# Loads and low parts reordered, the second norm in halves on PSUM, and sums formed in steps further apart, in a one-layer encoder kernel

## The chip, the core and the metric

The kernel runs on one core of one Trainium2 chip. The metric is the device time of one execution in microseconds; the figure quoted for a kernel is the median of several runs. Products run on TensorE (PE, with its weight loads PEld), elementwise work on VectorE (DVE) and ScalarE (ACT), a little on GpSimd (POOL), and DMAs are issued by SyncE (SP).

## The reference, cut to what matters

One layer of an encoder for 576 tokens (512 of a new stream, 64 of a running one), model width 2048, feed-forward width 5504, all in float32:

```
n = rms_norm(x, norm_mix_g)
q, k, va, u, vb = split(n @ w_in)                 # attention and gated MLP
h = x + concat([attend(q, k, va), gate(u, vb)]) @ w_out
n = rms_norm(h, norm_ffn_g)                       # the second norm
a, g = split(n @ w_up)                            # 2048 -> 2 x 5504
y = h + (silu(causal_dwconv3(a)) * g) @ w_down    # 5504 -> 2048

def rms_norm(x, g):
    return x * rsqrt(mean(x * x, axis=-1) + EPS) * g
```

## The kernel before

Everything is held transposed: 128 features on the partitions, the 576 tokens along the free axis, in two halves of 288 (`LEFT`, `RIGHT`). A row Y[k] is one such tile of 128 features, k from 0 to 15 for h. A product in float32 is made of three matmuls: each weight block and each operand is split into a high part (a cast, on ACT) and a low part (raw minus high, on DVE), and high by high, high by low and low by high are added up in PSUM. So a weight needs four steps: its DMA on SP's queue, the cast `hi` (L216), the subtraction `lo` (L217), and the matmuls.

The stages follow each other: first norm, attention and gated MLP to about 609 us; the out product to 816.6; the second norm to 829.3; a first part of the up product, called warm here, to 913; the rest of the up product to about 1800; the down product to the end.

The out product (jobs o0 to o11), the rest of the up product (jobs u3 to u42) and the down product (jobs d0 to d28) go through `strassen`. A job takes a two by two block of weights, 11, 12, 21 and 22, and forms seven products in place of eight, its units, in the order 1, 2, 6, 5, 7, 3, 4. They need sums of the blocks, made on DVE in place: s1 = 21 + 22 (L875), a21 = 11 - a21 (L878), a11 = s1 - a11 (L879), a12 = a12 - a11 (L882). The units 1, 6, 7 and 4 of a job write one PSUM bank (x), 2 another (y), 5 and 3 a third (z). So unit 6 may start only when `evict_sum` (L979) has read x of unit 1. The loop at the end of `strassen` writes its work in this order for unit i: prepare unit i + 1 (sums of blocks, cast, low part, and the next job's loads), the matmuls of unit i, the eviction of unit i - 1. A scheduler that goes by estimated costs then settles the order on each engine, and each engine works its queue in order. Pools with a few buffers (five for raw blocks, two each for high and low parts) decide when a load can start. The names below say it: lo_6_d11 is the low part of unit 6's weights in job d11, r0_d11 and r1_d11 are the two rows that the job adds to, x_d11 its bank.

The next job's blocks are loaded in the order 11 (in the preparation of unit 5), 12 (unit 7), 21 (unit 3), 22 (unit 4).

The second norm needs the sum of squares over the 2048 features. `out_done` squares each row Y[m] on ACT when its last job is evicted, and POOL adds it to `acc`. The last job, o11, gives the rows y_0 and y_1; then `rms_scale` splits `acc`, sums it over the partitions with four matmuls by ones, adds EPS and scales it (`ms`), and computes rsqrt by Ln, Exp and one Newton step on DVE (L294 to L299). The rows are normalised (`norm_n`, L710) and split into the units that the warm up product takes.

The warm part makes six 128-row pieces of the up product with plain triple products (`products`, L238), in groups: a_0, g_0 and a_1 together, for k = 0 to 15, then g_1, a_2 and g_2. Beside it, `form_sums` forms the sums of n's rows that the Strassen jobs need, for eight pairs of rows: per pair four sums on DVE (L727 to L730) and four splits (L543, L546). It is a generator: each `yield 2` lets two ticks go by, of which `products` gives one per step of k. `flush()` behind the last group runs what is left.

Of the kernel before, what the change touches and what calls it, by code (L numbers as in the profile page):

```python
# [8 lines left out]
F32 = mybir.dt.float32  # L9
# [6 lines left out]
P = 128  # L16
DM = 2048
# [54 lines left out]
def plan():  # L72

    k16 = list(range(KT))
    heads = []
    for h in range(NH):
        ms = [("v", h), ("k", h), ("q", h)]
        if h == 0:
            ms = [("k", h), ("v", h), ("q", h)]
            heads.append((ms, units_of(ms, k16, 6, (1, 2, 3))))  # L80
        else:
            heads += [([m], units_of([m], k16, 8)) for m in ms]
    seq = [("b", 0), ("b", 1), ("b", 2)]
    for g in range(3, NG):
        seq += [("u", g - 3), ("b", g)]
    seq += [("u", NG - 3), ("u", NG - 2), ("u", NG - 1)]
    gm = [([m], units_of([m], k16, 8)) for m in seq]
    ms = [("a", 0), ("g", 0), ("a", 1)]
    up = [(ms, units_of(ms, k16, 6))]
    rest = [(x, j) for j in range(WARM) for x in "ag"][2:]  # L90
    up += [([m], units_of([m], k16, 8)) for m in rest if m != ("a", 1)]
    return heads, gm, up
# [33 lines left out]
def layer(ctx: ExitStack, tc: tile.TileContext, xT, xg0, wst, cst, strip, ckT, cv, gws, cstate,  # L126
# [27 lines left out]
    ones = const.tile([P, P], F32R, name="ones")  # L154
    mhalf = const.tile([P, 8], F32, name="mhalf")
    qgs = const.tile([P, 1], F32, name="qgs")
    rx = const.tile([P, T], F32, name="rx")
# [42 lines left out]
    def load_raw(keys, name):  # L200
# [6 lines left out]
        return raw  # L207

    def split_raw(raw, n, name, fast=False):
        hi = wpool.tile([P, 8 * P], F32R, tag="hi", name=f"hi_{name}", bufs=2)  # L210
# [8 lines left out]

    def products(group, operand, pre=None, post=None, spare=False, then=None):  # L220

# [10 lines left out]
        last = {m: kt for u in units for m, kt in u}  # L232
        seen = set()

        def issue(ops):
# [5 lines left out]
        for ui, u in enumerate(units):  # L241
# [10 lines left out]
            for ti, (m, kt) in enumerate(u):  # L252
# [5 lines left out]
                fin = kt == last[m]  # L258
                issue([(m, j, w, x, st, sp)
                       for (w, x, st, sp) in ((wh, xh, first, False),  # L260
                                              (wh, xl, False, False),
                                              (wl, xh, False, fin))
                       for j in range(2)])
                tick()
# [79 lines left out]
    def constants():  # L344
        make_identity(nc, ident)
        nc.gpsimd.memset(ones_f, 1.0)
        nc.vector.tensor_copy(ones, ones_f)
        nc.gpsimd.memset(mhalf, -0.5)
        nc.sync.dma_start(cs, cst)
        nc.sync.dma_start(convst, cstate)  # L350
# [340 lines left out]
    squared = []  # L691

    def out_done(m):
        nc.sync.dma_start(hs[m], Y[m])
        if not squared:
            nc.scalar.activation(acc, Y[m], AF.Square)
        else:
            sq = big(f"sqy_{m}")[:, :T]
            nc.scalar.activation(sq, Y[m], AF.Square)
            nc.gpsimd.tensor_tensor(acc, acc, sq, ALU.add)  # L700
        squared.append(m)


    normed_n = set()

    def norm_n(k):
# [3 lines left out]
        nc.vector.scalar_tensor_tensor(Y[k], Y[k], col(C_GF + k), rx, ALU.mult, ALU.mult)  # L710
        for c, r in ((LEFT, 1 + k % 2), (RIGHT, 3 * (k % 2))):
            u = new_unit(("n", k // 2, r))
            unit_hi(u, Y[k][:, c])
            unit_lo(u, Y[k][:, c])

# [4 lines left out]
    def form_sums():  # L720

        tt = nc.vector.tensor_tensor
        for i in range(HP):
# [8 lines left out]
            for x, rr in ((ta, (5, 7)), (tb, (6, 4))):  # L732
                yield 2
                for r, c in zip(rr, (LEFT, RIGHT)):
# [96 lines left out]
    def strassen(jobs):  # L831
# [35 lines left out]
        def prep(i):  # L867
# [8 lines left out]
            elif r == 6:  # L876
                a11, a21 = R[job, "11"][:, :w], R[job, "21"][:, :w]
                tt(a21, a11, a21, ALU.subtract)  # L878
                tt(a11, R[job, "s1"][:, :w], a11, ALU.subtract)  # L879
# [3 lines left out]
            q = {1: "11", 2: "12", 6: "11", 5: "s1", 7: "21", 3: "12", 4: "22"}[r]  # L883
            HL[job, r] = split_raw(R[job, q], len(window(job)) + extra(job, r), f"{r}_{name}")
            nxt = {5: "11", 7: "12", 3: "21", 4: "22"}.get(r)
            at = i // len(ORDER) + 1
            if nxt and at < len(jobs):
                load(jobs[at], nxt)
                if r == 4:
                    load_res(jobs[at])  # L890

        def operand(job, k, r):
# [71 lines left out]
        def evict_sum(job, r, ps):  # L964
# [5 lines left out]
            dst = rs[m]  # L970
            end = job[0] == OUT and hi == HP
            if end and r in (2, 3, 7, 4):
                k = 2 * i + m
# [3 lines left out]
            if r == 4 and len(ps) == 4:  # L977
                tt(rs[1][:, RIGHT], ps[3], rs[1][:, RIGHT], ALU.add)
            tt(dst[:, c], src, rs[m][:, c], ALU.add)  # L979
            if r in (3, 4):  # L980
                if end:
# [35 lines left out]
        load_res(jobs[0])  # L1017
        prep(0)
        for i in range(len(work)):
            prep(i + 1)  # L1020
            mm(i)
            evict(i - 1)
            finish(i - 3)
            form(work[i][0])
# [7 lines left out]
    strassen([(OUT, v) for v in range(len(PLAN_O))])  # L1032
    for _ in rms_scale(rx, "h"):
        pass
    for i, grp in enumerate(up_plan):
        ps = products(grp, n_op, norm_n if i == 0 else None, spare=True)
        if i == 0:
# [88 lines left out]
```

## Time and profile before

| what | us |
| --- | --- |
| median of 3 runs | 2320.21 (2320.01 to 2320.77) |
| the profiled execution | 2321.35 |
| its span, first to last instruction | 2319.6 |
| TensorE busy | 2250.9 (97%) |
| VectorE busy | 1694.7 (73%) |
| ScalarE busy | 1003.5 (43%) |

The span is the time from the first to the last instruction of one profiled execution; the profiled execution's own time holds 1.75 us more. The page gives busy times over the whole span, so stages with different limits are mixed in them. Windows cut the span into stretches and give each engine's busy time and the clock granted to TensorE there (PEclk, 1.00 being 2.4 GHz). The waits name, for an engine's instructions, what ended the idle time before them. In a timeline each row is an instruction or several like ones in a row, with its start and length, and in brackets the idle time before it and its releaser.

### The profile page before, as it was taken

The numbers are of one execution on the slowest core, as the hardware profiler recorded it, in microseconds if no ns is written. First come the engines' busy times: TensorE is split into PE (matmuls) and PEld (weight loads), VectorE is DVE, ScalarE is ACT, GpSimd is POOL, SyncE is SP. The second block draws the span as 40 slices with busy tenths as digits, with TensorE's granted clock in tenths as the row PEclk, the third lists the DMA queues.
The fourth block names the chain that finished last, engine by engine and source line by source line (L and its number), as shares of the span: only waits on it lengthen the run. The fifth ranks groups of instructions, "written<-read, shape, count | busy, mean of one in ns | idle before, by whom it ended". The sixth has DMA issues, their size and how long they took to land.

```text
span 2319.6 us, 41325 instructions
## 1 busy us (share of the span) xinstructions
PE 2250.9 (97%) x16768; PEld 2233.3 (96%) x16768; DVE 1694.7 (73%) x2605; ACT 1003.5 (43%) x1485; POOL 207.8 (9%) x242
## 2 busy tenths in 40 slices
PE   7999999999999889999999999999999899999988
PEld 7999999999999779999999999999999899999988
DVE  7645655654787669777777777677777999978767
ACT  5444444432433345444444444444445444434332
POOL 4000000000002102111111111111111000000000
PEclk9999999999999889999999999999999999999999
DMA  6322222222344332333332333323333665545444
GB/s 211 102 92 92 97 94 80 83 84 78 119 152 138 127 103 92 103 125 105 104 117 93 123 106 103 120 91 122 107 102 123 210 195 173 188 161 179 157 146 141
DMA packets 107391, 286.24 MB, mean 123 GB/s; under 512 B 12096, under 2 KB 20416, under 8 KB 107200
## 3 DMA queue, kind: packets, MB, share of 16 engines
q1 hardware_dynamic: 107200, 283.60, 37.2%
q8 instruction: 132, 2.16, 0.4%
q14 instruction: 59, 0.48, 0.1%
HBM read 241.62 MB, written 41.93 MB: 122 GB/s over the span
## 4 chain that ended last, share of the span: by engine, by line
PE 64%; DVE 4%; DMA 2%; ACT 1%; issue 1%; POOL 0%; SPq 0%; ACTq 0%; DVEq 0%; POOLq 0%
PE x_u L911 7%; PE x_u L909 7%; PE x_u L913 7%; PE z_u L911 4%; PE z_u L909 4%; PE z_u L913 4%; PE x_d L909 3%; PE x_d L911 3%; PE x_d L913 3%; PE y_u L913 2%; PE y_u L911 2%; PE y_u L909 2%; PE ps_a L238 2%; PE z_d L909 2%; PE z_d L911 2%; PE z_d L913 2%
## 5 line engine op out<-in xcount | busy, mean ns | idle before, releaser
L216 ACT CAST hi_u<-raw_u 128x1024 fp32r<-128x1024 f32 x256 | 269.0, 1051 | 502.9 <-PE x_u L911 280.0
L217 DVE TENSOR_TENSOR lo_u<-raw_u,hi_u 128x1024 fp32r<-128x1024 f32 x256 | 312.9, 1222 | 223.0 <-ACT hi_u L216 222.5
L911 PE MATMUL x_u<-un_n,hi_u 128*128 128x288 f32 x1280 | 344.7, 296 | 0.0
L909 PE MATMUL x_u<-un_n,hi_u 128*128 128x288 f32 x1280 | 344.5, 295 | 0.0
L216 ACT CAST hi_d<-raw_d 128x896 fp32r<-128x896 f32 (+7 forms) x174 | 144.0, 828 | 249.0 <-PE x_d L911 104.7
L909 PEld LDWEIGHTS x_u<-un_n,hi_u 128*128 128x128 f32 x1280 | 242.1, 189 | 0.0
L911 PEld LDWEIGHTS x_u<-un_n,hi_u 128*128 128x128 f32 x1280 | 240.1, 188 | 0.0
L909 PE MATMUL x_d<-un_f,hi_d 128*128 128x288 f32 x672 | 185.5, 301 | 18.8 <-ACT hi_d L216 11.8
L913 PE MATMUL x_u<-un_n,lo_u 128*128 128x288 f32 x1280 | 195.2, 295 | 0.0
L911 PE MATMUL x_d<-un_f,hi_d 128*128 128x288 f32 x672 | 182.3, 296 | 0.0
L913 PEld LDWEIGHTS x_u<-un_n,lo_u 128*128 128x128 f32 x1280 | 178.4, 188 | 0.0
L217 DVE TENSOR_TENSOR lo_d<-raw_d,hi_d 128x896 fp32r<-128x896 f32 (+7 forms) x174 | 164.0, 943 | 17.5 <-ACT hi_d L216 16.4
L911 PE MATMUL z_u<-un_n,hi_u 128*128 128x288 f32 x640 | 172.2, 296 | 0.0
L909 PE MATMUL z_u<-un_n,hi_u 128*128 128x288 f32 x640 | 171.8, 295 | 0.0
L909 PEld LDWEIGHTS x_d<-un_f,hi_d 128*128 128x128 f32 x672 | 127.2, 189 | 25.1 <-ACT hi_d L216 19.8
L911 PEld LDWEIGHTS x_d<-un_f,hi_d 128*128 128x128 f32 x672 | 127.1, 189 | 0.0
L751 POOL COPY conv_new<-e 128x2 f32<-128x2 f32 x43 | 51.9, 1208 | 827.1 <-DVE e L954 766.3
L909 PEld LDWEIGHTS z_u<-un_n,hi_u 128*128 128x128 f32 x640 | 120.3, 188 | 0.0
L911 PEld LDWEIGHTS z_u<-un_n,hi_u 128*128 128x128 f32 x640 | 120.3, 188 | 0.0
L913 PE MATMUL x_d<-un_f,lo_d 128*128 128x288 f32 x672 | 108.3, 296 | 0.0
L216 ACT CAST hi_o<-raw_o 128x1024 fp32r<-128x1024 f32 (+7 forms) x72 | 54.9, 764 | 116.2 <-PE x_o L911 44.8
L913 PE MATMUL z_u<-un_n,lo_u 128*128 128x288 f32 x640 | 97.3, 294 | 0.0
(361 smaller groups left out, 5776.8 us busy)
## 6 DMA issues: line engine op xcount, KB each, us to landing
raw_u<-wst SPq DMA_DIRECT2D x176, 512.0 KB, 3.7
raw_d<-wst SPq DMA_DIRECT2D x56, 448.0 KB, 3.6
ac<-act SPq DMA_DIRECT2D x43, 288.0 KB, 3.6
ys<-r_d SPq DMA_DIRECT2D x42, 288.0 KB, 2.5
r_d<-ys SPq DMA_DIRECT2D x42, 288.0 KB, 3.1
raw_b<-wst SPq DMA_DIRECT2D x16, 512.0 KB, 3.2
raw_o<-wst SPq DMA_DIRECT2D x16, 512.0 KB, 3.6
raw_v<-wst SPq DMA_DIRECT2D x14, 512.0 KB, 3.2
```

Source lines behind the costliest of these rows:

```text
L216: nc.scalar.copy(hi[:, :w], raw[:, :w])
L217: nc.vector.tensor_tensor(lo[:, :w], raw[:, :w], f(hi[:, :w]), ALU.subtract)
L238: nc.tensor.matmul(out, w, x[j] if isinstance(x, tuple) else x[:, j * HF:(j + 1) * HF], start=st, stop=sp)
L751: nc.gpsimd.tensor_copy(conv_new[:, j, 0:2], e[:, 512:514])
L909: nc.tensor.matmul(out, w, u[:, 0], start=first and k == 0, stop=False, skip_group_check=True)
L911: nc.tensor.matmul(out, w, u[:, 1], start=False, stop=False, skip_group_check=True)
L913: nc.tensor.matmul(out, lo[:, k * P:(k + 1) * P], u[:, 0], start=False, stop=not add and k == n - 1, skip_group_check=True)
```

## The change

It makes five edits. The loads of the next job's blocks are written in the order 11 and 21 (unit 5), 22 (unit 7), 12 (unit 3). The low part is no longer formed with the cast but by `low`, behind the eviction, and a21 is formed there, behind the low part of unit 2. In the second norm the last two rows' squares don't pass through POOL: the sum of the other 14 rows is split and put into PSUM in the last out job, the squares of halves of y_0 and y_1 are split and added there by further matmuls, and Ln, Exp and Newton's step run on the right half behind unit 3 and on the left half behind unit 4, reading PSUM; an explicit load of the table set with Ln and Exp stands behind the eviction of unit 1. The first warm group takes k in the order 2 to 15, 0, 1, with the first step's right-half matmuls ahead. And `form_sums` lets three ticks go by in place of two in two of its three pauses.

```diff
@@ -88,3 +88,3 @@
     ms = [("a", 0), ("g", 0), ("a", 1)]
-    up = [(ms, units_of(ms, k16, 6))]
+    up = [(ms, units_of(ms, k16[2:] + k16[:2], 6))]
     rest = [(x, j) for j in range(WARM) for x in "ag"][2:]
@@ -208,2 +209,12 @@

+    def high_raw(raw, n, name):
+        hi = wpool.tile([P, 8 * P], F32R, tag="hi", name=f"hi_{name}", bufs=2)
+        nc.scalar.copy(hi[:, :n * P], raw[:, :n * P])
+        return hi
+    def low_raw(raw, hi, n, name):
+        lo = wpool.tile([P, 8 * P], F32R, tag="lo", name=f"lo_{name}", bufs=2)
+        nc.vector.tensor_tensor(lo[:, :n * P], raw[:, :n * P], f(hi[:, :n * P]), ALU.subtract)
+        return lo
     def split_raw(raw, n, name, fast=False):
@@ -219,3 +230,3 @@

-    def products(group, operand, pre=None, post=None, spare=False, then=None):
+    def products(group, operand, pre=None, post=None, spare=False, then=None, right=False):

@@ -233,2 +244,3 @@
         seen = set()
+        ops = []

@@ -258,7 +270,13 @@
                 fin = kt == last[m]
-                issue([(m, j, w, x, st, sp)
-                       for (w, x, st, sp) in ((wh, xh, first, False),
-                                              (wh, xl, False, False),
-                                              (wl, xh, False, fin))
-                       for j in range(2)])
+                ops += [(m, j, w, x, st, sp)
+                        for (w, x, st, sp) in ((wh, xh, first, False),
+                                               (wh, xl, False, False),
+                                               (wl, xh, False, fin))
+                        for j in range(2)]
+                if right and ui == 0:
+                    if ti < len(u) - 1:
+                        continue
+                    ops.sort(key=lambda op: -op[1])
+                issue(ops)
+                ops = []
                 tick()
@@ -692,4 +711,8 @@

+    SUMS, LASTROWS = [], PLAN_O[-1][0] * 2
     def out_done(m):
         nc.sync.dma_start(hs[m], Y[m])
+        if m // 2 == PLAN_O[-1][0]:
+            return
         if not squared:
@@ -702,2 +725,39 @@

+    def sum_squares():
+        sp = parts(acc, "h")
+        for j, c in enumerate((LEFT, RIGHT)):
+            SUMS.append(misc(f"cs{j}_h")[:, :HF])
+            for i in range(2):
+                nc.tensor.matmul(SUMS[j], ones, sp[i][:, c], start=i == 0, stop=False,
+                                 skip_group_check=True)
+    def more_squares(m, j):
+        c = (LEFT, RIGHT)[j]
+        sq = big(f"sq{j}_{m}")[:, :HF]
+        sp = tmpp.tile([P, 640], F32R, tag="tmp", name=f"sp{j}_{m}")
+        nc.scalar.activation(sq, Y[m][:, c], AF.Square)
+        split(sq, sp[:, LEFT], sp[:, RIGHT])
+        for i in range(2):
+            nc.tensor.matmul(SUMS[j], ones, sp[:, (LEFT, RIGHT)[i]], start=False,
+                             stop=i == 1 and m % 2 != j, skip_group_check=True)
+    def norm_half(j):
+        c = (LEFT, RIGHT)[j]
+        a, t = (big(f"{n}{j}_h")[:, :HF] for n in ("ms", "nw"))
+        y = rx[:, c]
+        nc.scalar.activation(y, SUMS[j], AF.Ln, scale=1.0 / DM, bias=epsc)
+        nc.scalar.activation(y, y, AF.Exp, scale=-0.5)
+        nc.vector.tensor_scalar(a, SUMS[j], 1.0 / DM, EPS, ALU.mult, ALU.add)
+        nc.vector.tensor_tensor(t, y, y, ALU.mult)
+        nc.vector.scalar_tensor_tensor(t, t, -0.5, a, ALU.mult, ALU.mult)
+        nc.vector.scalar_tensor_tensor(y, t, 1.5, y, ALU.add, ALU.mult)
+        for k in (2, 3):
+            normed_n.add(k)
+            nc.vector.scalar_tensor_tensor(Y[k][:, c], Y[k][:, c], col(C_GF + k), y,
+                                           ALU.mult, ALU.mult)
+            norm_unit(k, j)

@@ -710,6 +770,10 @@
         nc.vector.scalar_tensor_tensor(Y[k], Y[k], col(C_GF + k), rx, ALU.mult, ALU.mult)
-        for c, r in ((LEFT, 1 + k % 2), (RIGHT, 3 * (k % 2))):
-            u = new_unit(("n", k // 2, r))
-            unit_hi(u, Y[k][:, c])
-            unit_lo(u, Y[k][:, c])
+        for j in range(2):
+            norm_unit(k, j)
+    def norm_unit(k, j):
+        c, r = ((LEFT, 1 + k % 2), (RIGHT, 3 * (k % 2)))[j]
+        u = new_unit(("n", k // 2, r))
+        unit_hi(u, Y[k][:, c])
+        unit_lo(u, Y[k][:, c])

@@ -732,3 +796,3 @@
             for x, rr in ((ta, (5, 7)), (tb, (6, 4))):
-                yield 2
+                yield 3
                 for r, c in zip(rr, (LEFT, RIGHT)):
@@ -876,4 +940,3 @@
             elif r == 6:
-                a11, a21 = R[job, "11"][:, :w], R[job, "21"][:, :w]
-                tt(a21, a11, a21, ALU.subtract)
+                a11 = R[job, "11"][:, :w]
                 tt(a11, R[job, "s1"][:, :w], a11, ALU.subtract)
@@ -883,7 +946,9 @@
             q = {1: "11", 2: "12", 6: "11", 5: "s1", 7: "21", 3: "12", 4: "22"}[r]
-            HL[job, r] = split_raw(R[job, q], len(window(job)) + extra(job, r), f"{r}_{name}")
-            nxt = {5: "11", 7: "12", 3: "21", 4: "22"}.get(r)
+            n = len(window(job)) + extra(job, r)
+            hi = high_raw(R[job, q], n, f"{r}_{name}")
+            HL[job, r] = R[job, q], hi, n, f"{r}_{name}"
             at = i // len(ORDER) + 1
-            if nxt and at < len(jobs):
-                load(jobs[at], nxt)
+            if at < len(jobs):
+                for nxt in {5: ("11", "21"), 7: ("22",), 3: ("12",)}.get(r, ()):
+                    load(jobs[at], nxt)
                 if r == 4:
@@ -891,2 +956,14 @@

+        def low(i):
+            if i >= len(work):
+                return
+            job, r = work[i]
+            raw, hi, n, name = HL[job, r]
+            HL[job, r] = hi, low_raw(raw, hi, n, name)
+            if r == 2:
+                w = len(window(job)) * P
+                a21 = R[job, "21"][:, :w]
+                tt(a21, R[job, "11"][:, :w], a21, ALU.subtract)
         def operand(job, k, r):
@@ -979,2 +1057,11 @@
             tt(dst[:, c], src, rs[m][:, c], ALU.add)
+            if final:
+                if r == 1:
+                    tc.keep_in_program_order(
+                        nc.scalar.preload_act_table_set("natural_log_exp_and_others"))
+                    sum_squares()
+                elif r in (2, 3, 7, 4):
+                    more_squares(2 * i + m, int(c == RIGHT))
+                    if r in (3, 4):
+                        norm_half(int(r == 3))
             if r in (3, 4):
@@ -1018,2 +1105,3 @@
         prep(0)
+        low(0)
         for i in range(len(work)):
@@ -1022,2 +1110,3 @@
             evict(i - 1)
+            low(i + 1)
             finish(i - 3)
@@ -1032,6 +1121,5 @@
     strassen([(OUT, v) for v in range(len(PLAN_O))])
-    for _ in rms_scale(rx, "h"):
-        pass
     for i, grp in enumerate(up_plan):
-        ps = products(grp, n_op, norm_n if i == 0 else None, spare=True)
+        ps = products(grp, n_op, norm_n if i == 0 else None, spare=True,
+                      right=i == 0)
         if i == 0:
```

The hunks left out add the constant `epsc`, a tile filled with EPS, and `final`, true in the evictions of the out product's last job.

What becomes of the order is read from the instructions of each engine. First VectorE in the down product, job d11, before: raw_d11_11 and raw_d11_12 are the blocks turned into a11 and a12, un_f and fa belong to the sums of the down product's operand.

```order
L882 TENSOR_TENSOR raw_d11_12_21522<-raw_d11_12_21522,raw_d11_11_21492 128x896
L217 TENSOR_TENSOR lo_6_d11_21686<-raw_d11_11_21492,hi_6_d11_21685 128x896
L979 TENSOR_TENSOR r0_d11_21590<-x_d11_21649,r0_d11_21590 128x288
L546 TENSOR_TENSOR un_f_14_1_22139<-fa_14_21912,un_f_14_1_22139 128x288
L567 TENSOR_TENSOR fa_14_21912<-fa_14_21912 128x288
L217 TENSOR_TENSOR lo_5_d11_21720<-s1_d11_21643,hi_5_d11_21719 128x896
```

The same place of the changed kernel:

```order
L217 TENSOR_TENSOR lo_2_d11_21707<-raw_d11_12_21591,hi_2_d11_21679 128x896
L942 TENSOR_TENSOR raw_d11_11_21524<-s1_d11_21677,raw_d11_11_21524 128x896
L945 TENSOR_TENSOR raw_d11_12_21591<-raw_d11_12_21591,raw_d11_11_21524 128x896
L1057 TENSOR_TENSOR r0_d11_21622<-x_d11_21681,r0_d11_21622 128x288
L217 TENSOR_TENSOR lo_6_d11_21743<-raw_d11_11_21524,hi_6_d11_21719 128x896
L565 TENSOR_TENSOR un_f_14_1_22174<-fa_14_21947,un_f_14_1_22174 128x288
```

The eviction of unit 1 (r0_d11<-x_d11) moved ahead of lo_6_d11, and lo_2_d11 stands directly ahead of a11.

Next VectorE around the start of job u3, before: act_2 is the gating of the last warm group, and the blocks raw_u3 follow it.

```order
L773 TENSOR_TENSOR act_2_9836<-ps_g_2_0_9678,cv_2_9673 128x288
L774 TENSOR_TENSOR act_2_9836<-ps_g_2_1_9679,cv_2_9673 128x224
L775 TENSOR_TENSOR act_2_9836<-ps_g_2_1_9679,cv_2_9673 128x64
L217 TENSOR_TENSOR lo_2_u3_9856<-raw_u3_12_9843,hi_2_u3_9855 128x1024
L879 TENSOR_TENSOR raw_u3_11_9841<-s1_u3_9853,raw_u3_11_9841 128x1024
```

After, with ta, tb and un_n of the pairs 6 and 7, of which the first pair and the start of the second are shown:

```order
L837 TENSOR_TENSOR act_2_9834<-ps_g_2_0_9688,cv_2_9683 128x288
L838 TENSOR_TENSOR act_2_9834<-ps_g_2_1_9689,cv_2_9683 128x224
L839 TENSOR_TENSOR act_2_9834<-ps_g_2_1_9689,cv_2_9683 128x64
L791 TENSOR_TENSOR ta_6_9839<-y_12_8017 128x288
L792 TENSOR_TENSOR ta_6_9839<-y_13_8113,y_12_8017 128x288
L793 TENSOR_TENSOR tb_6_9840<-y_13_8113,ta_6_9839 128x288
L565 TENSOR_TENSOR un_n_6_5_9845<-ta_6_9839,un_n_6_5_9845 128x288
L794 TENSOR_TENSOR tb_6_9840<-y_13_8113,tb_6_9840 128x288
L565 TENSOR_TENSOR un_n_6_7_9848<-ta_6_9839,un_n_6_7_9848 128x288
L565 TENSOR_TENSOR un_n_6_6_9851<-tb_6_9840,un_n_6_6_9851 128x288
L565 TENSOR_TENSOR un_n_6_4_9854<-tb_6_9840,un_n_6_4_9854 128x288
L791 TENSOR_TENSOR ta_7_9857<-y_14_8336 128x288
```

Pairs 6 and 7, sixteen operations, came from ahead of the gating to behind it, and lo_2_u3 and a11 of u3 follow them.

Last VectorE from the end of the out product into the second norm, before: lo_a_0_0 and lo_a_0_1 are low parts of the first warm weights, sl_h the split of `acc`.

```order
L979 TENSOR_TENSOR y_0_8764<-z_o11_8710,r0_o11_8669 128x288
L217 TENSOR_TENSOR lo_a_0_0_8868<-raw_a_0_0_8865,hi_a_0_0_8867 128x768
L979 TENSOR_TENSOR y_1_8816<-x_o11_8708,r1_o11_8670 128x288
L217 TENSOR_TENSOR lo_a_0_1_8938<-raw_a_0_1_8935,hi_a_0_1_8937 128x768
L303 TENSOR_TENSOR sl_h_8841<-acc_91,sh_h_8840 128x576
L361 TENSOR_SCALAR ms_h_8850<-cs0_h_8844 128x288
L361 TENSOR_SCALAR ms_h_8850<-cs1_h_8845 128x288
L297 TENSOR_TENSOR nw_h_8855<-rx_90 128x576
L298 SCALAR_TENSOR_TENSOR nw_h_8855<-nw_h_8855,ms_h_8850 128x576
L299 SCALAR_TENSOR_TENSOR rx_90<-nw_h_8855,rx_90 128x576
L710 SCALAR_TENSOR_TENSOR y_0_8764<-y_0_8764,cs_81,rx_90 128x576
```

And after, where sp1_0 is the low part of the right half of row 0's squares, cs1_h the bank with the right half's sum, and sp0_1 that of the left half of row 1's squares:

```order
L1057 TENSOR_TENSOR y_1_8834<-x_o11_8708,r1_o11_8670 128x288
L217 TENSOR_TENSOR lo_4_o11_8843<-raw_o11_22_8637,hi_4_o11_8820 128x512
L321 TENSOR_TENSOR sp1_1_8837<-sq1_1_8836,sp1_1_8837 128x288
L1057 TENSOR_TENSOR y_0_8775<-z_o11_8710,r0_o11_8669 128x288
L228 TENSOR_TENSOR lo_a_0_0_8916<-raw_a_0_0_8913,hi_a_0_0_8915 128x768
L321 TENSOR_TENSOR sp1_0_8859<-sq1_0_8858,sp1_0_8859 128x288
L1057 TENSOR_TENSOR y_1_8834<-x_o11_8708,r1_o11_8670 128x288
L228 TENSOR_TENSOR lo_a_0_1_8972<-raw_a_0_1_8969,hi_a_0_1_8971 128x768
L753 TENSOR_SCALAR ms1_h_8865<-cs1_h_8755 128x288
L754 TENSOR_TENSOR nw1_h_8866<-rx_91 128x288
L755 SCALAR_TENSOR_TENSOR nw1_h_8866<-nw1_h_8866,ms1_h_8865 128x288
L321 TENSOR_TENSOR sp0_1_8884<-sq0_1_8883,sp0_1_8884 128x288
```

The operations on 576 columns became operations on 288, the right half's chain begins behind y_1's last eviction and one more low part, and sp0_1 stands in it.

## Rows read from the trace of the kernel before

**Rows 1.** The page: busy us of each engine, share, instructions.

```profile
PE 2250.9 (97%) x16768; PEld 2233.3 (96%) x16768; DVE 1694.7 (73%) x2605; ACT 1003.5 (43%) x1485; POOL 207.8 (9%) x242
```

**Rows 2.** Windows: us, busy time (instructions) per engine, PEclk, DMA, GB/s.

```profile
900.00:1800.00 900.00, 900.00 (x6795) 900.00 (x6794) 672.65 (x847) 411.06 (x516) 129.22 (x160) 1.00 0.33 109
829.29:836.59 7.30, 7.30 (x36) 7.24 (x37) 7.30 (x17) 4.00 (x11) 0.00 (x0) 0.62 0.00 0
886.00:889.40 3.40, 2.92 (x12) 2.92 (x13) 3.40 (x10) 1.53 (x4) 0.00 (x0) 0.50 0.76 257
```

**Rows 3.** Waits of PE, 600 to 830 us: us in total, times, longest.

```profile
PE x_o L909 <- ACT hi_o L216: 13.0, 7, 5.1
PE ps_a L238 <- ACT un_n L543: 7.1, 1, 7.1
PE cs_h L289 <- ACT sh_h L302: 4.0, 1, 4.0
PE x_o L909 <- DVE r_o L979: 4.0, 5, 1.6
```

**Rows 4.** Waits of PE, 1800 to 2320 us.

```profile
PE x_d L909 <- ACT hi_d L216: 11.8, 10, 2.5
PE x_d L909 <- DVE r_d L979: 6.4, 8, 1.3
```

**Rows 5.** Timeline, PE: start, us, engine, line, operation [idle before <-releaser].

```profile
886.48 0.85 PE L238 MATMUL ps_a<-un_n,lo_a 128*128 128x288 f32 x2 [2.82 <-DVE lo_a L217]
```

**Rows 6.** Timeline, job u3, the last products of its second unit.

```profile
918.24 1.23 PE L913 MATMUL y_u<-un_n,lo_u 128*128 128x288 f32 x8
```

**Rows 7.** Timeline, 814 to 831 us, out product's end, second norm.

```profile
815.39 0.95 DVE L217 TENSOR_TENSOR lo_a<-raw_a,hi_a 128x768 fp32r<-128x768 f32 x1
...
816.60 0.46 DVE L979 TENSOR_TENSOR y<-x_o,r_o 128x288 f32<-128x288 f32 x1 [0.27 <-PE x_o L913]
...
823.56 1.28 ACT L295 ACT_TABLE_LOAD   x1
824.86 0.68 ACT L295 ACTIVATE rx<-rx 128x576 f32<-128x576 f32 x1
...
827.16 0.76 DVE L299 SCALAR_TENSOR_TENSOR rx<-nw_h,rx 128x576 f32<-128x576 f32 x1
827.95 1.55 DVE L710 SCALAR_TENSOR_TENSOR y<-y,cs,rx 128x576 f32<-128x576 f32 x2
828.80 1.49 ACT L543 CAST un_n<-y 128x288 fp32r<-128x288 f32 x4 [3.27 <-DVE y L710]
...
829.29 1.24 PE L238 MATMUL ps_a<-un_n,hi_a 128*128 128x288 f32 x3 [7.08 <-ACT un_n L543]
```

**Rows 8.** Timeline, the out product's last job, ACT.

```profile
806.15 0.62 ACT L216 CAST hi_o<-raw_o 128x512 fp32r<-128x512 f32 x1 [3.59 <-DVE raw_o L879]
```

**Rows 9.** Timeline of VectorE around the start of u3.

```profile
906.74 0.45 DVE L727 TENSOR_TENSOR ta<-y 128x288 f32<-128x288 f32 x1
...
907.85 1.22 DVE L217 TENSOR_TENSOR lo_u<-raw_u,hi_u 128x1024 fp32r<-128x1024 f32 x1
...
910.83 1.22 DVE L875 TENSOR_TENSOR s_u<-raw_u,raw_u 128x1024 f32<-128x1024 f32 x1
...
914.26 1.22 DVE L217 TENSOR_TENSOR lo_u<-raw_u,hi_u 128x1024 fp32r<-128x1024 f32 x1
```

**Rows 10.** Timeline, job d11, third unit's start.

```profile
2006.63 0.45 DVE L979 TENSOR_TENSOR r_d<-x_d,r_d 128x288 f32<-128x288 f32 x1
...
2007.23 0.37 PE L909 MATMUL x_d<-un_f,hi_d 128*128 128x288 f32 x1 [0.70 <-DVE r_d L979]
```

**Rows 11.** Timeline, a job of the up product, third unit's low part and products.

```profile
1006.20 1.22 DVE L217 TENSOR_TENSOR lo_u<-raw_u,hi_u 128x1024 fp32r<-128x1024 f32 x1
...
1010.42 1.23 PE L913 MATMUL x_u<-un_n,lo_u 128*128 128x288 f32 x8
```

**Rows 12.** Timeline of VectorE, job o8.

```profile
753.37 2.12 DVE L875 TENSOR_TENSOR s_o<-raw_o,raw_o 128x1024 f32<-128x1024 f32 x1 [1.75 <-DMA raw_o<-wst]
```

More of the change, by code (lines that the diff above doesn't have):

```diff
@@ L155, in layer @@
     mhalf = const.tile([P, 8], F32, name="mhalf")
+    epsc = const.tile([P, 1], F32, name="epsc")
     qgs = const.tile([P, 1], F32, name="qgs")
@@ L348, in constants @@
         nc.gpsimd.memset(mhalf, -0.5)
+        nc.gpsimd.memset(epsc, EPS)
         nc.sync.dma_start(cs, cst)
@@ L971, in evict_sum @@
             end = job[0] == OUT and hi == HP
+            final = end and job == jobs[-1]
             if end and r in (2, 3, 7, 4):
```

## The prediction

> **What bounds the kernel now.** First the page: TensorE is busy for 2250.9 of 2319.6 us [rows 1], so ending all its waits would win 68.7 us. The windows then show where nothing can be won: from 900 to 1800 us, the up product, TensorE is busy all the time at a granted clock of 1.00, and VectorE for 672.65 of the 900 us [rows 2]. There the change can only lose. The waits of TensorE, read next, name what ends its idle time in the other stages. In the out product and second norm, 600 to 830 us, it is 13.0 us for the cast of a weight, 4.0 us for an eviction, and 4.0 and 7.1 us in the norm [rows 3]; in the down product 11.8 us for casts and 6.4 us for evictions [rows 4]. The timelines, read last, say what each wait hung on. Idle time has a second price: the 36 products behind the gap in the norm took 7.30 us at a mean granted clock of 0.62 [rows 2], and the stretch with the gap of 2.82 us [rows 5] and what follows it ran at 0.50 [rows 2], which is 1.2 of 2.4 GHz. At the full clock eight products take 1.23 us, the last of them 0.29 by itself, so their pitch is (1.23 - 0.29) / 7 = 0.13 us [rows 6]; at half it is twice that.
>
> **1. The second norm.** Before, the last eviction starts at 816.60 [rows 7], just when the out product's last matmul has ended (I call that moment T). Behind it come a square, POOL's addition, the split, four matmuls of sums, Ln, a table load of 1.28, Exp, three VectorE operations of 0.76 each, two of 0.78, a cast, and the next product at 829.29 [rows 7]: T + 12.7. The first weights' 36 products end 7.30 later [rows 2], at T + 20.0.
>
> After, the sum of 14 rows goes into PSUM while the last job still runs, the two last rows are added there by TensorE, and the right half's chain hangs on an eviction one unit earlier. What comes after T, with 0.45 for a VectorE operation on 288 columns [rows 10] (0.37 where one follows another) and 0.4 for one on ACT (four casts take 1.49 [rows 7]): the right sums done at T + 0.9; Ln 1.35, Exp 1.75; the mean, which stands behind a low part of 0.95 [rows 7], 1.95; then three operations, a low part among them, and the sums of the left half's last square, until the norm's factor is there at 4.0; row 2 at 4.4; its cast at 4.75, seen by TensorE at T + 5.2. The operands of the left half follow at T + 8.2 to 9.4, and I expect the clock at half again, so that the 36 products take 7.3 as before and end at T + 12.5: 7.5 us earlier. Against it, there are 12 matmuls of sums in place of four, and four of the twelve stand in the idle time: 8 x 0.13 = 1.1 us. Net -6.4 us; -4.4 if the chain is 2 us longer, -8.5 if the clock comes back at once.
>
> The table load now stands on ACT between two casts of the last job. Those took 0.62 [rows 8]; cast, load, cast is 0.6 + 1.3 + 0.6 = 2.5 us, and TensorE, which starts on the first, has four sums and 12 products until it wants the second: 0.6 + 16 x 0.13 = 2.7. So it is hidden by 0.2 us, and costs 0. In the trace Exp starts 0.02 us after the end of its table load (823.56 + 1.28, then 824.86) [rows 7]. The Trainium skill ("ScalarE: Activation LUTs", What ACT_TABLE_LOAD costs) counts a drain of about 1.38 us to each switch beside the load, 2.66 in all. No such time stands behind the load in the trace; by the page the second cast would be late and the sum below 1.2 us less of a gain.
>
> **2. The steps further apart.** A pair's eight VectorE operations run from 906.74 to 910.83 with a low part of 1.22 among them [rows 9], so they take 2.9 us. Before, pair 2's were ahead of the low part of a_2, for which TensorE waited 2.82 us [rows 5]. Now that low part is ahead of them: -2.8, and the 12 matmuls in the 3.40 us at half clock [rows 2] get back 12 x 0.13 = 1.5: -4.3. But eight steps a pair make 64, more than the groups up to g_2 have, and so pairs 6 and 7 are formed in the flush behind them, ahead of lo_2 of job u3 on VectorE, which started at 914.26 before [rows 9]. It now starts 2 x 2.9 = 5.8 later and is there at 914.3 + 5.8 + 1.2 = 921.3. TensorE wants it at 918.24 [rows 6]: a wait of 3.1 us. Queued behind lo_2 are a11 (1.2) and then ACT's cast for the next unit (1.0), which TensorE wants eight products (1.1) after lo_2: 1.1 more. As the 2.82 us did, this wait should bring the half clock, about 1 us of it beside the second wait: together +5.2 (between 3.1, where neither follows, and 6.5; 0 if the pairs' operations find time before g_2 ends). Net of both about +1.
>
> **3. Evictions ahead of low parts.** A job's third unit shares its bank with the first, so TensorE must wait for the first's eviction. In job d11 that starts at 2006.63 behind a low part, and TensorE starts at 2007.23 after 0.70 idle [rows 10]. The order has the eviction first now, earlier by a low part, some 1.07 us (1.22 for 1024 columns [rows 9], here 896): the wait goes. Of the 8 such waits, 6.4 us [rows 4], I leave 0.9 for a job of one row-pair, too short for either order, and 0.5 for a rest: -5.0 (bounds 0 and -6.4). Of the 5 in the out product, 4.0 us [rows 3], I take -3.0 (0 and -4.0). The low part comes 0.45 later, but it is wanted only 16 products, 2.1 us, after its unit's start; that time hides it.
>
> The up product has the same edit 40 times, with no wait to end. There a low part starts at 1006.20 and takes 1.22, and its products start at 1010.42 [rows 11]; three operations of about 0.37 each may now go ahead of it, which leaves 2 us. Cost 0; were that cover gone, each 0.1 us would be 4 us.
>
> **4. Loads.** The sum s1 needs the blocks 21 and 22, third and fourth before. In job o8 it started only at 753.37, after 1.75 idle for a load [rows 12]. Now 22 is third and 12 last, and s1 can start some 1.5 us earlier; but lo_2, which needs 12, now stands ahead of a21 and a11 in the chain to the third unit's cast. I take -1.0 in all (of the 13.0 and 11.8 us for casts [rows 3, 4] the rest stays; bounds -5 and +2, since residual loads also go ahead of raw blocks on SP in a few jobs).
>
> **Sum.** -6.4 - 4.3 + 5.2 - 5.0 - 3.0 - 1.0 = -14.5 us. The profiled execution took 2321.35 us (its span and 1.75 around it); its like would take 2306.9. It was 1.1 above the runs' median, 2320.21, from which the same sum gives 2305.7. I say 2306.
>
> **The rivals.** (a) No stall in u3, because the pairs end before it matters: -14.5 - 5.2 = -19.7, 2300.5. For it, VectorE has idle time before g_2 ends; against it, VectorE runs in order, and 16 operations stand ahead of lo_2. (b) Evictions and loads give nothing, for whatever waited for an eviction then waits for a cast or a low part: the sum without 5.0, 3.0 and 1.0 is -5.5, 2314.7. For it, the casts are the larger rows; against it, the wait in d11 ended with the eviction alone. (c) The norm gains little, for the products start at T + 5.2 and then stand still for the left half: 4 us less, -10.5, 2309.7. For it, the left half's factor ends 3 us after the right one's; against it, 18 products at half clock fill just that. (d) Slower: in the up product low parts, queued behind evictions that themselves wait for TensorE, come after they are wanted. It decides once the delay is over 2 us a unit; at 0.5 us beyond that in each of 40 jobs it is +20, with the rest +5.5, 2325.7. For it, VectorE is busy for three quarters of that stretch; against it, TensorE never waits there now [rows 2].
>
> **Chances.** The forecast 0.57, (a) 0.10, (b) 0.14, (c) 0.12, (d) 0.07. The forecast's own range is 2302 to 2311; to hold 8 in 10, 2299 (case (a) with a somewhat better norm) to 2315 (case (b)). A change under 0.2%, 4.6 us, can't be told from none here. Faster: the forecast, (a), (c) and half of (b), 0.57 + 0.10 + 0.12 + 0.07, less 0.03 for their tails, 0.83; same, the rest of these, 0.10; slower, which is (d), 0.07.
>
> **What would show it.** In the profile after: products 5 to 6 us after the out product, and no table load between Ln and Exp; no wait for lo_a at 886; a wait of 3 us for lo_u in u3; TensorE's waits for r_o and r_d down to about 1 us each, those for hi_d about as before; nothing from 925 to 1800. Waits for lo_u in many jobs, evictions still waited for, or products starting later than T + 8 would make the prediction wrong.

## The result, and the profile after

The changed kernel takes 2298.4 us (median of 4 runs, 2297.95 to 2299.23), before 2320.26; the ratio is 0.9906 (95% interval 0.9889 to 0.9923), 21.9 us less. The forecast was 2306, its range 2299 to 2315: the direction was right, the gain half as large again, and the time 0.6 us below the range. The profiled execution has a span of 2296.3 us, 23.3 less than before.

The first and the last matmul of each stage cut the traces into stretches. The last three columns are experiments with one edit alone, told below (us). Each column is one profile: the changed kernel profiled a second time gave 202.26 for the out product and 504.24 for the down product.

| stretch | before | changed | loads alone | low parts alone | norm alone |
| --- | --- | --- | --- | --- | --- |
| out product | 206.98 | 201.15 | 200.13 | 202.26 | 206.73 |
| its end to the 36th warm product | 20.30 | 12.48 | 19.82 | 19.86 | 11.83 |
| from there to u3 | 76.08 | 71.77 | 74.80 | 74.80 | 74.81 |
| job u3 | 22.37 | 27.33 | 22.37 | 22.37 | 22.38 |
| rest of the up product | 867.98 | 866.16 | 867.98 | 867.98 | 866.16 |
| down product | 512.62 | 503.66 | 505.84 | 507.43 | 514.45 |

TensorE's waits in the changed kernel's out product and norm (us in total, times, longest):

```profile
PE x_o L986 <- ACT hi_o L212: 4.3, 6, 1.1
PE y_o L986 <- ACT hi_o L212: 2.5, 2, 1.8
...
PE ps_a L250 <- ACT un_n L562: 1.4, 1, 1.4
PE y_o L990 <- DVE lo_o L217: 1.3, 1, 1.3
```

Against [rows 3], the 4.0 us for evictions (r_o) are gone altogether, those for casts of the units that write the bank x fell from 13.0 to 4.3, and there are new waits for the second unit's cast and low parts (y_o), whose block 12 is now loaded last. The 7.1 us for un_n became 1.4. The same in the down product:

```profile
PE x_d L986 <- ACT hi_d L212: 9.5, 10, 3.1
PE y_d L986 <- ACT hi_d L212: 3.0, 2, 1.9
PE z_d L990 <- DVE lo_d L217: 1.2, 1, 1.2
PE y_d L990 <- DVE lo_d L217: 0.7, 1, 0.7
```

Against [rows 4], the 6.4 us for evictions are gone, and the 11.8 for casts are still 9.5, with 3.0 for the second unit. The rows sum to 14.4 where they summed to some 20, and the stretch is 9.0 us shorter: more than the rows.

The norm, from the last eviction to the first product:

```profile
810.98 0.46 DVE L1057 TENSOR_TENSOR y<-x_o,r_o 128x288 f32<-128x288 f32 x1
...
811.46 0.50 ACT L751 ACTIVATE rx<-cs_h,epsc 128x288 f32<-128x288 f32 x1 [0.18 <-PE cs_h L743]
...
811.99 0.44 ACT L752 ACTIVATE rx<-rx 128x288 f32<-128x288 f32 x1
...
814.30 0.95 DVE L759 SCALAR_TENSOR_TENSOR y<-y,cs,rx 128x288 f32<-128x288 f32 x2
...
815.27 0.75 ACT L562 CAST un_n<-y 128x288 fp32r<-128x288 f32 x2
...
815.74 0.61 PE L250 MATMUL ps_a<-un_n,hi_a 128*128 128x288 f32 x1 [1.39 <-ACT un_n L562]
```

It answers to [rows 7]: the last eviction starts at 810.98, Ln 0.48 later, the next product 4.76 later, where it was 12.69. No table load stands between Ln and Exp. The load stands here on ACT, in the last job:

```profile
799.49 0.62 ACT L212 CAST hi_o<-raw_o 128x512 fp32r<-128x512 f32 x1 [0.92 <-DVE raw_o L942]
800.13 1.28 ACT L1061 ACT_TABLE_LOAD   x1
801.42 0.62 ACT L212 CAST hi_o<-s_o 128x512 fp32r<-128x512 f32 x1
```

The cast behind the load starts at 801.42, as the load ends (800.13 + 1.28).

The new wait in u3, VectorE, TensorE and ACT:

```profile
896.38 0.23 DVE L839 TENSOR_TENSOR act<-ps_g,cv 128x64 f32<-128x64 f32 x1
...
902.40 1.23 DVE L217 TENSOR_TENSOR lo_u<-raw_u,hi_u 128x1024 fp32r<-128x1024 f32 x1
...
903.69 2.29 PE L990 MATMUL y_u<-un_n,lo_u 128*128 128x288 f32 x8 [3.05 <-DVE lo_u L217]
...
904.86 1.05 ACT L212 CAST hi_u<-raw_u 128x1024 fp32r<-128x1024 f32 x1 [2.34 <-DVE raw_u L942]
```

The gating ends behind 896.38, the pairs' sixteen operations take until lo_2 starts at 902.40, and TensorE, which was ready for it, waits 3.05 us. Before, lo_2 stood right behind the gating in VectorE's order, and started at 914.26 [rows 9].

### The profile page after: what moved, and what is told of

Same layout as the page of the kernel before. It is cut to its first block, busy times and chain, and to the rows that moved or that the text cites. A ratio compares the mean times of both kernels' runs of the same rounds, so it can differ in the third digit from the quotient of the medians.

```text
span 2296.3 us, 41253 instructions
## 1 busy us (share of the span) xinstructions
PE 2247.0 (98%) x16776; PEld 2232.5 (97%) x16776; DVE 1705.1 (74%) x2614; ACT 999.2 (44%) x1492; POOL 206.7 (9%) x241
## 4 chain that ended last, share of the span: by engine, by line
PE 92%; DVE 4%; DMA 1%; issue 1%; ACT 1%; SPq 0%; ACTq 0%; DVEq 0%
PE x_u L986 7%; PE x_u L990 7%; PE x_u L988 7%; PE ps_b L250 4%; PE ps_u L250 4%; PE ps_q L250 4%; PE ps_k L250 4%; PE ps_v L250 4%; PE z_u L990 4%; PE z_u L988 4%; PE z_u L986 4%; PE x_d L986 4%; PE x_d L988 4%; PE x_d L990 4%; PE y_u L990 2%; PE z_d L986 2%
## 5 line engine op out<-in xcount | busy, mean ns | idle before, releaser
L217 DVE TENSOR_TENSOR lo_u<-raw_u,hi_u 128x1024 fp32r<-128x1024 f32 x240 | 292.8, 1220 | 134.1 <-ACT hi_u L212 134.1
L212 ACT CAST hi_u<-raw_u 128x1024 fp32r<-128x1024 f32 x240 | 251.1, 1046 | 304.4 <-PE z_u L988 148.8
```

The source lines that it names most:

```text
L212: nc.scalar.copy(hi[:, :n * P], raw[:, :n * P])
L217: nc.vector.tensor_tensor(lo[:, :n * P], raw[:, :n * P], f(hi[:, :n * P]), ALU.subtract)
```

## The experiments

Each timed kernel was compared with the kernel before on its own chip, and the chips differ by a few us (medians of before: 2320.3, 2322.3 to 2322.6, and 2326.3), so the ratios are what to compare: 0.9906 for the changed kernel, 0.001 being 2.3 us. Run again on another chip, the changed kernel gave 0.9885, so a comparison of two chips is good to some 5 us; on one chip it is closer.

The out and the down product gave more than forecast. Theory 1: the eviction edit was sized too small, by what a wait costs beside its row. Theory 2: the load order did it, since s1 and with it all of VectorE's queue waited for block 22. Theory 3: the two work only together.

**Low parts back with the cast.**

```diff
-            HL[job, r] = R[job, q], hi, n, f"{r}_{name}"
+            HL[job, r] = hi, low_raw(R[job, q], hi, n, f"{r}_{name}")
...
-            low(i + 1)
```

> The changed kernel with one edit taken back: low parts (and a21) are formed with the cast again, ahead of the eviction. Changed kernel 2298.4, before 2320.3. Theory 1 (the eviction edit was sized too small, since a wait costs TensorE its row in the trace plus some 0.25 us to drain and restart, and 13 waits of 10.4 us went): +12 to +14, 2310 to 2312, and TensorE's waits for r_o and r_d return, about 13 of them, 10 us. Theory 2 (the load order gave what the sum lacked): +8, 2306, with the same waits back. Theory 3 (the two edits only work together): +14 or more here, and as much when the loads are taken back.

Measured: 0.9904 (0.9891 to 0.9918), 2300.5: no slower than the changed kernel's 0.9906, and some 4 us slower than its 0.9885. Four waits each for r_o and r_d came back, 2.8 and 4.1 us, while those for casts and low parts are smaller. All three theories had this edit dearer, at 8 to 14 us; theory 1 falls, and what the edit is worth lies under what this comparison of two chips can tell.

**Loads back in the old order.**

```diff
-                for nxt in {5: ("11", "21"), 7: ("22",), 3: ("12",)}.get(r, ()):
+                for nxt in {5: ("11",), 7: ("12",), 3: ("21",), 4: ("22",)}.get(r, ()):
```

> The changed kernel with the loads of the next job's blocks in the old order 11, 12, 21, 22. Theory 1: +1 to +3, 2299 to 2301: the waits for casts in o8, o10 and o11 (13.0 us before, 6.8 after) come back in part, those for evictions stay at 0. Theory 2: +8 or more, 2306. Theory 3: +10 or more.

Measured: 0.9940 (0.9926 to 0.9953), some 8 us slower than the changed kernel's 0.9906 and some 13 slower than its 0.9885, as theory 2 has it. The edit that I had sized at 1 us is the large one.

**One edit alone on the kernel before**: low parts, then loads.

> The kernel before with one edit: low parts (and a21) behind the eviction; old load order, old norm, old steps. Theory 1 (the order on VectorE is what TensorE's waits for evictions hang on): -8 or more, 2312. Theory 2 (they hang on the loads: the sum s1 waits on VectorE for block 22, 14.9 + 7.8 us of such waits before and 1.6 + 1.7 after, and all that stands behind s1 is late, the eviction too): about -1, within 3 of before, 2317 to 2321, with VectorE's waits for loads at some 20 us as before; the rows for r_o and r_d may go, but those for casts grow by as much.

Measured: 0.9974 (0.9963 to 0.9984), 2317.5 against 2322.3. TensorE's waits in the down product, for casts and for evictions:

```profile
PE x_d L984 <- ACT hi_d L212: 13.7, 12, 2.9
...
PE x_d L984 <- DVE r_d L1055: 0.5, 1, 0.5
```

So the order on VectorE does end the waits for evictions, as forecast, and it is worth some 5 to 6 us, not 8 or more as theory 1 had it, nor 1 as theory 2 had it: waits for casts are larger than in [rows 4]. (The profile is of the shortest of twelve runs, 2310 to 2320, so its two stretches in the table flatter this edit.) VectorE's own waits for loads are in sum what they were, 23.9 us against 22.7:

```profile
DVE s_d L937 <- DMA raw_d<-wst: 19.8, 19, 1.9
...
DVE s_o L937 <- DMA raw_o<-wst: 4.1, 5, 1.6
```

> The kernel before with one edit: the next job's blocks loaded in the order 11, 21, 22, 12. Theory 2: -9 to -12, 2308 to 2311, VectorE's waits of s_d and s_o for loads near 3 us in all, out product about 5 shorter and down product about 7 shorter. Theory 1: -1, 2319. Theory 3 (the two edits only work together): both this one and the one with low parts alone stay within 3 of before.

Measured: 0.9939 (0.9925 to 0.9953), 2308.7 against 2322.3, 14 us, more than the 9 to 12 of theory 2; out product 6.9 and down product 6.8 us shorter. VectorE's waits for loads, then TensorE's for casts and evictions:

```profile
DVE s_d L937 <- DMA raw_d<-wst: 2.5, 3, 1.6
...
DVE s_o L937 <- DMA raw_o<-wst: 1.6, 2, 1.1
```

```profile
PE x_d L973 <- ACT hi_d L212: 6.6, 8, 2.5
PE x_o L973 <- ACT hi_o L212: 4.5, 5, 2.7
PE x_d L973 <- DVE r_d L1044: 4.0, 4, 1.3
...
PE y_o L973 <- ACT hi_o L212: 2.8, 1, 2.8
PE x_o L973 <- DVE r_o L1044: 2.8, 4, 1.6
...
PE y_d L973 <- ACT hi_d L212: 2.1, 2, 1.8
```

Most of the gain is in the waits for casts into bank x: 24.8 us in [rows 3, 4] and 11.1 here; the second unit's casts, whose block now comes last, bring 4.9 back. The loads alone also end about a third of the time waited for evictions [rows 3, 4], and half of such waits in the down product, though here the low part still stands ahead of the eviction on VectorE. Theory 2 holds in the main; theory 3 falls, since each edit gains alone, and together they gain less than the sum.

**Is it the order, or that the loads are written a unit earlier?**

```diff
-                for nxt in {5: ("11", "21"), 7: ("22",), 3: ("12",)}.get(r, ()):
+                for nxt in {5: ("11", "12"), 7: ("21",), 3: ("22",)}.get(r, ()):
```

> The changed kernel with the loads written at the new places in the program (two behind unit 5, one behind 7, one behind 3) but in the old order 11, 12, 21, 22. If the place in the order matters (s1 needs 21 and 22, and block 22 comes last again): as with the loads taken back, 0.994 of before, some 8 us over the changed kernel, VectorE waiting some 20 us for loads. If it matters that they are written a unit earlier: as the changed kernel, 0.9906.

Measured: 0.9930 (0.9916 to 0.9944); on the same chip the changed kernel, run again, gave 0.9885 (0.9871 to 0.9900). So it is the order: some 10 us slower, and VectorE waits for loads again:

```profile
DVE s_d L939 <- DMA raw_d<-wst: 19.1, 18, 2.0
...
DVE s_o L939 <- DMA raw_o<-wst: 4.4, 7, 1.9
```

> The changed kernel once more, on the chip and beside the runs that the next kernels share. All theories: 0.9906 of before.

Measured: 0.9885, 2299.6 against a before of 2326.3 on this chip.

**The old second norm in the changed kernel, and the new one alone.** Both take whole functions from the one or the other; the diff is the norm's part of the change.

> The changed kernel with the old second norm (sum on POOL, one chain over both halves, old order of k). Theory 1: what the trace shows of the norm's stretch, -7.9 after the out product's end, less 8 matmuls of sums, 1.1, in the last job: +6.8, 2305.2. Rival: the sums in the last job held up more than their own length (two waits of about 1 us for casts of sh_h and of the last job stand there), so that taking the norm back costs only +5, 2303.4.

Measured: 0.9928 (0.9915 to 0.9940), 2306.3; against the changed kernel's 0.9906 that is 5 us, against its 0.9885 10, with the old waits of 7.1 and 4.0 us. Its first products come 12.55 us after the out product, and its up product took 867.98.

> The kernel before with the new second norm (with its order of k) alone. Stretch from the out product's end to the 36th product -7.9, sums in the last job +1.1: -6.8; and the up product 866.2 long in place of 868.0, as in all kernels with this norm, -1.8. Together -8.6, 0.9963 of before. Rival: in the old order the last job has no room for the sums, and they cost 2 us more: 0.997.

Measured: 0.9945 (0.9933 to 0.9957), nearly 13 us less than before, where its stretches in the table add up to 10, the edge of the interval. More than the 8.6 forecast, then, and the profiled executions agree on some 10: with the old norm the changed kernel's span is 10.2 us longer (2306.5 against 2296.3), and this one's is 9.3 shorter than before's (2310.3 against 2319.6).

**The steps.**

```diff
-                yield 3
+                yield 2
```

> The changed kernel with form_sums letting two ticks go by in each pause again. The two stretches measured -4.3 (the wait at 886 gone) and +5.0 (the new wait in u3), so theory 1: the wait of 3.05 us for lo_2 of u3 goes, a wait of about 2.8 for lo_a of a_2 comes back, net -0.7, 2297.7. Rival: without the flush u3 gains 5 and the wait for lo_a does not return, since the norm's halves left VectorE earlier: 2293.5.

Measured: 0.9892 (0.9879 to 0.9905). The wait in u3 is gone and the old one is back:

```profile
PE ps_a L250 <- DVE lo_a L228: 2.8, 1, 2.8
```

So the steps move a wait from one place to another, -4.3 and +5.0, and no slowdown shows in the kernel without them. Keeping both ends needs 46 ticks for eight pairs:

```diff
-                yield 3
+                yield 3 if i < 2 else 2
...
-            yield 2
+            yield 2 if i < 2 else 1
```

> The changed kernel with form_sums' pauses at 3, 3, 2 ticks for the first two pairs and 2, 2, 1 for the other six, 46 in all, so that the low part of a_2 stays ahead of pair 2 and yet all pairs are formed before the flush. Theory 1 of the steps (they move two waits): neither the wait at 886 (2.8 us) nor the one in u3 (3.05) is there, warm -4.3 and u3 -5 against the changed kernel's +5.0: 5 us under the changed kernel, 0.9906 - 0.0021 = 0.9885 of before. Rival: the pairs, denser now, hold up another low part of the warm groups, and half of it comes back: 0.9895.

Measured: 0.9868 (0.9853 to 0.9882), 2291.3: the fastest kernel of all. Again, beside the changed kernel:

> The steps 3, 3, 2 for two pairs and 2, 2, 1 for six once more, beside the changed kernel. By the stretch in u3 (+0.75 in place of +4.96) and the warm one (-3.6 in place of -4.3): 3.5 us under the changed kernel, 0.989 of before. If the full clock that its out product showed belongs to it: 8 to 9 us under, 0.987.

Measured: 0.9867 (0.9855 to 0.9880), 2295.0 against 2299.6 for the changed kernel on the same chip, 4.6 us less: nearer to the 3.5 of the stretches than to the 8 to 9 of the clock. All four of its runs are shorter than all four of the changed kernel, though the intervals overlap. What remains of both waits:

```profile
PE ps_g L250 <- ACT hi_g L227: 0.4, 1, 0.4
```

```profile
PE x_u L986 <- ACT hi_u L212: 0.4, 1, 0.4
```

Both are 0.4 us. With low parts back at the cast, beside it:

> The same steps as in the kernel beside it (3, 3, 2 twice, then 2, 2, 1), and low parts formed with the cast again. Against that kernel it prices the eviction edit with the loads in the new order. Theory 1: 8 us slower than it or more. Theory 2: 1 us slower, within 2 of it, with waits for r_o and r_d of some 7 us where that one has more for casts and low parts.

Measured: 0.9878 (0.9863 to 0.9893), 2294.2 against 2291.3 on the same chip: with the loads in the new order the low parts are worth some 3 us, which these intervals do not yet separate from none.

## Why the forecast was wrong

**The norm: right.** The product came at T + 4.8 where I had counted T + 5.2, the 36 products ended 7.8 us earlier (forecast 7.5), and the 8 more sums are in the out product. The table load cost nothing, as the rows before had it; the drain of 1.38 us that the Trainium skill ("ScalarE: Activation LUTs", What ACT_TABLE_LOAD costs) adds to each switch shows nowhere: 0.02 us lie between the cast before the load and the load, 0.01 between the load's end and the next cast.

**The steps: the old wait and the new one right, the exact sizes by luck.** -4.3 was forecast and -4.3 measured, +5.2 and +5.0, of that 3.05 the wait (forecast 3.1). The second wait, of 1.1 us for the next cast, didn't come: at half the clock (0.50 granted) the unit's eight products took 2.29 us, and the cast was there at 905.91, just ahead of their end. In its place the first wait cost 1.9 us beside its row, where I had counted 1. Nor does a wait cost the same in every profile. The stretch with the old wait of 2.8 us took 76.08 us at a granted clock of 0.98 in the profile of before, 74.80 at 1.00 in each of the three experiments of the table, and 77.55 at 0.96 in the changed kernel with two ticks: 3.0 to 5.8 us more than the 71.8 without that wait. Job u3 with the new wait was 4.9 to 6.3 us longer in the six profiles that have it. I had taken the price of the clock from one profile.

**The step that failed is the loads, "-1.0 in all".** Loads and low parts were to give 9.0 us, 8.0 of them by the low parts; the out product gave 5.8 and 1.1 more for the sums that it took in, and the down product 9.0: 15.9. The loads alone give 14, the low parts alone 5 to 6. I had let the waits for casts stay nearly as they were; the loads alone take those into bank x from 24.8 to 11.1 us. For the evictions I had read TensorE's waits and followed one of them a single step back, to an eviction behind a low part, and stopped at that order. VectorE's own waits, which I did not weigh, have the rest. Before:

```profile
DVE s_d L875 <- DMA raw_d<-wst: 14.9, 20, 1.6
...
DVE s_o L875 <- DMA raw_o<-wst: 7.8, 4, 3.2
```

After:

```profile
DVE s_o L939 <- DMA raw_o<-wst: 1.7, 1, 1.7
DVE s_d L939 <- DMA raw_d<-wst: 1.6, 2, 1.1
```

Job d11 shows how such a wait reaches TensorE. VectorE before, ahead of the eviction in [rows 10]:

```profile
1998.34 1.09 DVE L875 TENSOR_TENSOR s_d<-raw_d,raw_d 128x896 f32<-128x896 f32 x1 [1.09 <-DMA raw_d<-wst]
1999.35 1.09 DVE L217 TENSOR_TENSOR lo_d<-raw_d,hi_d 128x896 fp32r<-128x896 f32 x1
...
2005.63 1.09 DVE L217 TENSOR_TENSOR lo_d<-raw_d,hi_d 128x896 fp32r<-128x896 f32 x1
```

s1 starts after 1.09 us of waiting for block 22, the fourth load, and from there VectorE never stops until the eviction at 2006.63, for which TensorE waits 0.70 us. So 1.09 us less at the head of that queue could be more than TensorE's whole wait. The same job with the loads' edit alone, VectorE and TensorE, shows that it is:

```profile
1986.75 1.08 DVE L937 TENSOR_TENSOR s_d<-raw_d,raw_d 128x896 f32<-128x896 f32 x1
...
1994.13 1.09 DVE L217 TENSOR_TENSOR lo_d<-raw_d,hi_d 128x896 fp32r<-128x896 f32 x1
...
1995.14 0.45 DVE L1044 TENSOR_TENSOR r_d<-x_d,r_d 128x288 f32<-128x288 f32 x1
...
1995.96 0.29 PE L973 MATMUL x_d<-un_f,hi_d 128*128 128x288 f32 x1
```

s1 has no wait ahead of it, the low part still stands ahead of the eviction, and TensorE goes on to the third unit at 1995.96 with no idle time. With the low parts' edit alone s1 waits 1.30 us, and TensorE doesn't wait either: here each edit is enough by itself. The same job in the changed kernel:

```profile
1979.93 1.09 DVE L939 TENSOR_TENSOR s_d<-raw_d,raw_d 128x896 f32<-128x896 f32 x1
...
1987.24 0.45 DVE L1057 TENSOR_TENSOR r_d<-x_d,r_d 128x288 f32<-128x288 f32 x1
1987.61 1.08 DVE L217 TENSOR_TENSOR lo_d<-raw_d,hi_d 128x896 fp32r<-128x896 f32 x1
```

s1 starts at 1979.93 with no wait ahead of it, since 22 is the third load and had landed at 1977.4, 2.9 us ahead of the fourth (1980.3); the eviction (1987.24) now stands ahead of the low part (1987.61). The third load and the fourth are issued 2.7 to 2.8 us apart and land 2.8 to 2.9 us apart in both kernels, so the third place in place of the fourth is worth that step to whoever needs the block. I had seen the idle time ahead of s1 in o8 [rows 12] and priced it for that job; twenty jobs of the down product have it too, and what stands behind s1 is not one chain to a cast but all of VectorE's queue.

**The low parts were priced too high in their turn**, -8.0 where they give 5 to 6 alone and 0 to 4 once the loads come in the new order. There they do what rival (b) said: of the down product's waits, 4.1 us for evictions went, and those for casts and low parts rose from 8.5 us, with the low parts at the cast, to 14.5 (the stretch is 1.1 us shorter all the same). For the loads rival (b) was wrong.

**The price of a wait was too low as well.** TensorE in d11 before, around the wait of 0.70 us [rows 10]:

```profile
2005.72 0.81 PE L913 MATMUL y_d<-un_f,lo_d 128*128 128x288 f32 x5
...
2007.44 0.30 PE L911 MATMUL x_d<-un_f,hi_d 128*128 128x288 f32 x1
```

The last of the five started at 2005.72 + 4 x 0.13 = 2006.24. At full pitch the next but one would have started 0.26 later, at 2006.50; it started at 2007.44. So the wait cost 0.94 us, 0.24 more than its row says: 0.16 because the row counts from the end of a matmul (0.29) and not from the pitch (0.13), and 0.08 because the first one after it holds the second up. I summed rows. It is no peculiarity of d11: of the 23 gaps of this stretch that stand alone and end at the full clock, 22 cost 0.23 to 0.27 us beyond their row; behind one of 2.52 us the granted clock was 0.50, and by the ninth product after it 1.2 us beyond the row were lost. Thirty-two gaps of TensorE in the down product became nineteen, so 13 x 0.24 = 3.1 of its 9.0 us stand in no row; the idle time itself fell by 5.5, from 20.2 to 14.8.

**The up product** gave 1.8 us where I had forecast nothing. Its instructions' order changed in all kernels with the new low parts, yet it took 867.98 us in each kernel with the old norm, the one with low parts alone included, and 866.2 in each with the new norm. So the gain, 0.28 ns a matmul over 6553 of them, comes with the norm's edit and not with the low parts; rival (d) was wrong in sign too. What in the norm does it isn't settled: where the operands lie in memory may have moved, and no run separated that.

## What to carry to other kernels

When the matrix engine waits for another engine's result, follow that engine's queue backward past the instruction that delivered, to the last time it idled: what ended that idle time is a cause to test by itself, beside the order of the last few instructions. Price each wait of TensorE at its row plus 0.24 us (at this tile's size, and more where the clock falls behind it), since fewer waits pay even where the rows' sum stays. And work that is spread out over more steps must still end ahead of the stage that needs its engine: what a flush collects returns as one block at the worst place.

## What the runs showed that I had not expected

The clock's part in one profile is large and does not belong to an edit. The changed kernel and the one with 3, 3, 2 and 2, 2, 1 ticks differ only behind the out product; in it, TensorE, VectorE and ScalarE have the same instructions in the same order. Windows of their out products (us, busy per engine, PEclk), first the changed kernel with its up product:

```profile
609.79:810.94 201.15, 189.87 (x1353) 185.22 (x1353) 165.88 (x257) 86.33 (x133) 19.97 (x13) 0.97 0.46 151
922.52:1788.68 866.16, 866.16 (x6553) 866.16 (x6552) 647.26 (x806) 387.07 (x488) 121.64 (x156) 1.00 0.32 110
```

And the other, with a second profile of it:

```profile
609.85:806.69 196.84, 184.26 (x1353) 179.57 (x1353) 165.18 (x257) 86.37 (x133) 20.89 (x13) 1.00 0.47 154
```

```profile
609.91:810.05 200.14, 187.16 (x1353) 182.54 (x1353) 165.08 (x257) 86.56 (x133) 19.98 (x13) 0.98 0.47 151
```

Its first profile has less clock taken away than the changed kernel's (1.00 for 0.97) and a stretch 4.3 us shorter, though its TensorE idled longer in it (12.6 for 11.3 us). In its second profile the clock was 0.98 and the stretch 3.3 us longer than in its first. So a stretch of one profile with waits in it is known to some 4 us, and an edit of that size needs the timed runs, or a stretch like the up product, which came out at 866.2 or 868.0 us in every kernel.
